# The first MLP product of a mixer block by Strassen's algorithm: seven 256-token block products per pair of column tiles in place of eight

## The chip, the cores and the metric

The kernel runs on one core of one Trainium2 chip. The metric is the device time of one execution in microseconds (us), as the median of several runs. The engines are named as in the profile: PE is TensorE (its matmuls), PEld the loading of weights into TensorE, DVE is VectorE, ACT is ScalarE, POOL is GpSimd, and SP is SyncE, which here issues the weight loads from HBM (DMAs).

## The reference

The reference is one layer of a hybrid block on x of 512 tokens by 1024 channels, in float32: four mixer branches, gates, an output projection, and then an MLP. The change touches only the MLP, which is

```python
h2 = rms_norm(x, norm_mlp_pre)          # 512 x 1024
u = jax.nn.relu(h2 @ w_mlp_in)          # w_mlp_in: 1024 x 4096
x = x + rms_norm((u * u) @ w_mlp_out, norm_mlp_post)
```

## The kernel before

Activations are kept transposed, channels on the 128 partitions and tokens along the free axis. The contraction over 1024 channels is thus 8 blocks of 128, numbered k, and `KD` is 8.

**Float32 by three matmuls.** Every operand is split in two, a rounded part `hi` and the rest `lo` (`split`: ACT casts `hi` on L157, DVE subtracts to get `lo` on L160). A product is then three matmuls, hi·hi, hi·lo and lo·hi (`mm3`, L256 to L258). The split of the normalised activation h2 is `h2h` and `h2l`, both kept in SBUF for all 512 tokens.

**The first MLP product.** `w_mlp_in` is taken in 32 tiles of 128 columns, numbered m. SP loads a tile (`raw`, 512 KB, four buffers), ACT and DVE split it into `whi` and `wlo` (three buffers each), and PE runs 8 k times 3 matmuls of 128 by 128 weights against all 512 tokens, 24 matmuls into one PSUM bank. `act_sq` follows: ACT applies Relu out of PSUM (L1117), and POOL squares in place (L1118). Results go to tiles `u2` of SBUF, eight m to a tile. The first four tiles (`NHALF`) are done in two halves of 256 tokens, because the last 128 tokens are still being normalised: first all four tiles on tokens 0 to 255, then all four on tokens 256 to 511.

**The late normalisation.** `norm_split` makes h2 from one 128-token block. For the last block (`late`) the order is: ACT sums the squares (L281), PE transposes the unscaled block (L293), ACT computes `rstd` (L273, L274), PE spreads `rstd` (L301), DVE scales (L304), ACT casts `h2h` (L306) and DVE subtracts `h2l` (L307).

**The second MLP product** (`rowproj` with `u_split`) takes u² back from the `u2` tiles, splits it two m at a time, and streams rows of `w_mlp_out`.

The order on each engine is not written out by hand around the change. It follows the order of the code, moved by a scheduler according to priorities, and buffers come from pools in rotation (`bufs`).

Of the kernel before, what the change touches and what calls it, by code (L numbers as in the profile page):

```python
# [120 lines left out]
def hybrid_mixer_kernel(ctx, tc, I, out):  # L121
# [15 lines left out]
    def ps_acc():  # L137
        return psp.tile([P, 512], F32, name="acc", tag="acc", bufs=2)
# [96 lines left out]
    def w_split(rv, where=None, eng=dve):  # L235
        wp, wb, tag = where or (wpool, 3, "w")
        hi = wp.tile([P, 1024], F32R, name="whi", tag=tag + "hi", bufs=wb)
        lo = wp.tile([P, 1024], F32R, name="wlo", tag=tag + "lo", bufs=wb)
        shape = rv.shape
        n = 1  # L240
        for d in shape[1:]:
            n *= d
        if len(shape) == 3:
            hv = hi[:, 0:n].rearrange("p (k c) -> p k c", k=shape[1])
            lv = lo[:, 0:n].rearrange("p (k c) -> p k c", k=shape[1])
        else:
# [27 lines left out]
        act.activation(out=r, in_=r, func=AF.Exp, scale=-0.5)  # L274
        return r

    def norm_split(src, gain, dh, dl, t, sq, late=False, first=None):


        ssq = tiny("ssq")  # L280
        a0 = act.activation(out=sq, in_=src, func=AF.Square, accum_out=ssq)  # L281
        r = rms_cols(ssq, D, "rstd")
        if not late:
            d0 = dve.tensor_scalar(out=sq, in0=src, scalar1=r, scalar2=None, op0=ALU.mult)
            if first:
# [729 lines left out]
    def m_tile(name, dt):  # L1015
        return mpool.tile([P, KD, S], dt, name=name, tag="mbig", bufs=2)
# [34 lines left out]
    def big2(name, dt):  # L1051
        return ph2.tile([P, KD, S], dt, name=name, tag="big2", bufs=2)
# [50 lines left out]
    def fin1(t, ps):  # L1103
        post_norm(ps, gpost, x1[:, t])
        sq = ph2.tile([P, D], F32, name="y", tag="y", bufs=2)
        norm_split(x1[:, t], V_MLP, h2h, h2l, t, sq, t == NT - 1)

    spare, uspl = (ph2, NSPARE, "w"), (ph2, 2, "u")
    rowproj(I["w_out"][0], KD, TAIL1, lambda k: (mh[:, k], ml[:, k]),
# [8 lines left out]
        pool.tensor_tensor(out=dst, in0=dst, in1=dst, op=ALU.mult)  # L1118

    w1 = I["w_mlp_in"][0]  # L1120
    for m in range(DFF // P):
        if m % 8 == 0:
            u2.append(big2("u2", F32) if m < 16 else m_tile("u2b", F32))
        if m < NHALF:
            continue
        if m == NHALF:
            first = [(ps_sm() if a else ps_acc(), w_split(raw_cols(w1, a * P), spare if a == 3 else None)) for a in range(NHALF)]
            for half in range(2):
                for a in range(NHALF):
                    proj(first[a][1], h2h, h2l, slice(256 * half, 256 * half + 256), first[a][0], half == 0)  # L1130
            for a in range(NHALF):
                act_sq(first[a][0], a)
# [79 lines left out]
```

## Time and profile before

| what | value |
| --- | --- |
| median of 3 runs | 885.64 us |
| lowest and highest run | 885.21 and 886.63 us |
| the profiled execution, its time | 884.56 us |
| the profiled execution, its span | 882.9 us |
| mean granted TensorE clock | 0.999 of full speed |

The span runs from the first to the last instruction of the profiled execution, and 1.7 us of its time lie around it. The profiled execution is 1.08 us under the median. "Granted clock" is the share of full TensorE speed that the throttle allowed. In the rows of a trace, times are us from the start of the span, and a matmul's shown duration includes the time until its last result, so that consecutive matmuls overlap in it.

### The profile page before, as it was taken

What the parts mean: (1) busy time and instruction counts of PE and PEld (TensorE: products, weight loads), DVE (VectorE), ACT (ScalarE), POOL (GpSimd) and SP (SyncE); (2) the same over time, 40 slices, a digit from 0 to 9 for tenths busy, and PEclk for the clock granted to TensorE, in tenths of its full rate; (3) what the DMA queues carried; (4) which work ended last, traced back from release to release, by engine and by line L of the source; (5) the groups of instructions that cost most, each with busy time, mean ns of one, the idle gap of its engine ahead of it and who ended that gap; (6) DMA issues with size and microseconds to landing.
All of it is one profiled execution on the core that took longest, in us unless ns stands there. A gap on an engine that the chain in (4) does not pass through costs nothing.

```text
span 882.9 us, 11119 instructions
## 1 busy us (share of the span) xinstructions
PE 866.5 (98%) x4407; PEld 712.9 (81%) x4407; DVE 437.9 (50%) x705; ACT 391.9 (44%) x667; POOL 117.7 (13%) x113
## 2 busy tenths in 40 slices
PE   7999999999999999999999999999999999999997
PEld 6987778987777778888888789888888888888885
DVE  6488798446885775344435575222222333333334
ACT  6346653425996755544443454322222332222222
POOL 3200020110000003022214002232222200000000
PEclk9999999999999999999999999999999999999999
DMA  8333253601220113333323803333333433333202
GB/s 264 102 104 95 60 114 89 128 25 52 67 85 26 48 48 97 96 95 96 97 95 110 271 27 93 96 96 96 97 96 101 128 106 99 104 96 103 75 1 95
DMA packets 123667, 83.24 MB, mean 94 GB/s; under 512 B 19472, under 2 KB 115744, under 8 KB 123616
## 3 DMA queue, kind: packets, MB, share of 16 engines
q1 hardware_dynamic: 117696, 77.03, 30.0%
q10 hardware_dynamic: 5696, 4.73, 1.7%
q0 software_dynamic: 224, 0.79, 0.3%
q8 instruction: 34, 0.56, 0.3%
q14 instruction: 17, 0.14, 0.1%
HBM read 79.63 MB, written 2.88 MB: 93 GB/s over the span
## 4 chain that ended last, share of the span: by engine, by line
PE 87%; DVE 6%; ACT 2%; POOL 2%; DMA 2%; issue 1%; ACTq 0%; SPq 0%; DVEq 0%; POOLq 0%
PE acc L258 53%; PE b L258 24%; PE b L817 2%; DVE wlo L160 1%; DVE qkvT L440 1%; PE b L847 1%; PE b L838 1%; DMA raw<-in_w_out_dram 1%; ACT whi L157 1%; PE b L646 1%; DMA raw<-in_w_in_dram 1%; PE b L293 1%; POOL gate L1042 1%; POOL wlo L160 1%; DVE dec L483 0%
## 5 line engine op out<-in xcount | busy, mean ns | idle before, releaser
L160 DVE TENSOR_TENSOR wlo<-raw,whi 128x1024 fp32r<-128x1024 f32 x134 | 171.6, 1284 | 257.7 <-ACT whi L157 257.5
L157 ACT CAST whi<-raw 128x1024 fp32r<-128x1024 f32 x136 | 142.8, 1053 | 274.6 <-PE acc L258 237.8
L258 PE MATMUL acc<-hh,wlo 128*128 128x512 f32 x368 | 145.8, 396 | 0.8 <-DVE wlo L160 0.8
L258 PE MATMUL acc<-hh,whi 128*128 128x512 f32 x368 | 146.2, 397 | 0.0
L258 PE MATMUL acc<-hl,whi 128*128 128x512 f32 x368 | 145.1, 394 | 0.0
L258 PE MATMUL acc<-h2l,whi 128*128 128x512 f32 (+1 forms) x240 | 91.7, 382 | 0.0
L258 PE MATMUL acc<-h2h,whi 128*128 128x512 f32 (+1 forms) x240 | 91.7, 382 | 0.0
L258 PE MATMUL acc<-h2h,wlo 128*128 128x512 f32 (+1 forms) x240 | 91.7, 382 | 0.0
L258 PEld LDWEIGHTS acc<-hh,wlo 128*128 128x128 f32 x368 | 69.2, 188 | 16.5 <-issue 1.6
L258 PEld LDWEIGHTS acc<-hh,whi 128*128 128x128 f32 x368 | 69.2, 188 | 14.9 <-issue 1.6
L258 PEld LDWEIGHTS acc<-hl,whi 128*128 128x128 f32 x368 | 69.2, 188 | 13.8 <-issue 0.4
L258 PE MATMUL b<-wlo,whi 128*128 128x512 f32 x192 | 74.7, 389 | 0.0
L258 PE MATMUL b<-whi 128*128 128x512 f32 x192 | 74.7, 389 | 0.0
L258 PE MATMUL b<-whi,wlo 128*128 128x512 f32 x192 | 74.6, 390 | 0.0
L258 PEld LDWEIGHTS acc<-h2h,whi 128*128 128x128 f32 x240 | 45.1, 188 | 8.8
L258 PEld LDWEIGHTS acc<-h2h,wlo 128*128 128x128 f32 x240 | 45.1, 188 | 8.7
L258 PEld LDWEIGHTS acc<-h2l,whi 128*128 128x128 f32 x240 | 45.1, 188 | 8.7
L1042 POOL TENSOR_TENSOR gate<-gate 128x512 f32<-128x512 f32 x16 | 22.6, 1418 | 198.2 <-DVE gate L1040 198.2
L258 PEld LDWEIGHTS b<-whi,wlo 128*128 128x128 f32 x192 | 36.0, 188 | 7.9 <-DVE wlo L160 0.4
L258 PEld LDWEIGHTS b<-whi 128*128 128x128 f32 x192 | 36.0, 188 | 7.5
L258 PEld LDWEIGHTS b<-wlo,whi 128*128 128x128 f32 x192 | 36.0, 188 | 7.4
L1118 POOL TENSOR_TENSOR u<-u 128x512 f32<-128x512 f32 x16 | 25.7, 1606 | 110.2 <-ACT u L1117 110.1
(322 smaller groups left out, 1461.2 us busy)
## 6 DMA issues: line engine op xcount, KB each, us to landing
raw<-in_w_gate_dram SPq DMA_DIRECT2D x32, 512.0 KB, 3.9
raw<-in_w_mlp_in_dram SPq DMA_DIRECT2D x32, 512.0 KB, 4.1
raw<-in_w_mlp_out_dram SPq DMA_DIRECT2D x32, 512.0 KB, 3.5
raw<-in_w_in_dram SPq DMA_DIRECT2D x23, 512.0 KB, 3.7
raw<-in_w_branch_up_dram SPq DMA_DIRECT2D x8, 512.0 KB, 3.8
raw<-in_w_out_dram SPq DMA_DIRECT2D x8, 512.0 KB, 3.5
x_t<-in_x_dram SPq DMA_DIRECT2D x4, 512.0 KB, 7.6
x<-in_x_dram ACTq DMA_DIRECT2D x1, 2048.0 KB, 11.9
```

The lines of the kernel that those rows point to most:

```text
L157: c = act.copy(out=hi, in_=src)
L160: eng.tensor_tensor(out=lo, in0=src, in1=hi.bitcast(F32), op=ALU.subtract)
L258: pe.matmul(out=ps, lhsT=a, rhs=b, start=first and i == 0, stop=last and i == 2, skip_group_check=True)
L293: pe.transpose(out=ps[:, k * P:(k + 1) * P], in_=(src if late else sq)[:, ks], identity=ident)
L440: dve.scalar_tensor_tensor(out=y[:, sh:], in0=ps[:, 0:S - sh], scalar=vec(V_CONV + 6 * j + m), in1=y[:, sh:], op0=ALU.mult, op1=ALU.add)
L646: pe.matmul(out=pv[:, j], lhsT=av[h][:, j], rhs=src[:, j], start=j == 0, stop=j == NT - 1, skip_group_check=True)
L817: pe.matmul(out=ps[:, at_[j]:at_[j] + n], lhsT=qT[e][0:rows, j * P:n], rhs=kT[e][0:rows, 0:n], start=j == js[0], stop=j == js[-1], skip_gr ...
L838: pe.transpose(out=pst[:, k * P:(k + 1) * P], in_=pr[:, k * P:(k + 1) * P], identity=ident)
L847: made.append(pe.matmul(out=psb[C * e:C * e + C, i * P:(i + 1) * P], lhsT=vt(k, 2 * p + e), rhs=pts[e][:, at_[j] + k * P:at_[j] + (k + 1) ...
L1042: pool.tensor_tensor(out=g, in0=g, in1=gts[4 * m + i - 1], op=ALU.add)
L1118: pool.tensor_tensor(out=dst, in0=dst, in1=dst, op=ALU.mult)
```

## The change

The 32 column tiles are now: four in two halves as before, tiles 4 and 5 as before (`NPLAIN = 6`), and the other 26 as 13 pairs. A pair of tiles (256 columns of the weights) and the 1024 channels in two halves make the weights a 2 by 2 matrix of blocks (`A[i][k]`, i the tile, k the half of the channels, each 512 channels by 128 columns), and h2 in two halves of channels and two halves of tokens is another (`B`, each 512 channels by 256 tokens). Their product takes eight block products in the plain way, and seven with Strassen's form with 15 sums: four sums of weight blocks (S1 to S4), four of activation blocks (T1 to T4, made once), and seven that combine products.

- h2 is now kept in float32 as well (`h2f`, a new argument `full` of `norm_split`), for all tokens. T1 to T4 are made from it in place, and each is split like any operand.
- For each pair, DVE makes S1 to S4 in place in the two `raw` tiles. A11 and A12, the two blocks of the first tile, are split together (`x`); A22 is split into a `y` buffer (`yw`); the four S are split two to a `whi`/`wlo` buffer.
- A block product is `part`: 4 k times 3 matmuls on 256 tokens, 12 matmuls. PE's order for one pair is p1 with A11, p6 (S2·T2), p5 (S1·T1), p1 again with A12 into the same bank, p7 (S3·T3), p3 (S4·B11), and p7 again with A22·T4 into the same bank.
- Five sums of products are DVE instructions that read PSUM: `sa`, `sb` and three of the four output blocks `o`. ACT copies p1 to `s1` in SBUF before p1 is continued, and applies Relu to each block. `s1`, `sa`, `sb` and `o[1][1]` have high priority in the scheduler.
- The square of u for these 26 tiles is on ACT (`Square`, one instruction for a tile) instead of POOL.

```diff
@@ norm_split
-    def norm_split(src, gain, dh, dl, t, sq, late=False, first=None):
+    def norm_split(src, gain, dh, dl, t, sq, late=False, first=None, full=None):
-            dst = sq[:, 512 * g:512 * g + 512].rearrange("p (k c) -> p k c", k=4) if late else pv
+            dst = (full[:, 4 * g:4 * g + 4, t * P:(t + 1) * P] if full is not None else
+                   sq[:, 512 * g:512 * g + 512].rearrange("p (k c) -> p k c", k=4) if late else pv)
...
+    diff(B[0][0], B[0][1], B[0][0])
+    T1 = rows_split(B[0][0], uspl)
+    diff(B[0][1], B[1][1], B[0][1])
+    diff(B[1][1], B[1][1], B[0][0])
+    T2 = rows_split(B[1][1], uspl)
+    T3 = rows_split(B[0][1], spare)
+    diff(B[1][0], B[1][0], B[1][1])
+
+    for m in range(NHALF, NPLAIN):
         act_sq(proj(w_split(raw_cols(w1, m * P)), h2h, h2l), m)
+    T4 = rows_split(B[1][0], spare)
...
+    def part(ps, w, t, start=True):
+        for k in range(KH):
+            mm3(ps, w[0][:, k], w[1][:, k], t[0][:, k], t[1][:, k], start and k == 0, k == KH - 1)
...
+        x = wt("x")
+        split(x[0], x[1], r[0])
+        z_ = ph2.tile([P, D], F32R, name="yw", tag="y", bufs=2).rearrange("p (z k c) -> p z k c", z=2, k=KH)
+        z = (z_[:, 0], z_[:, 1])
+        split(z[0], z[1], A[1][1])
+        diff(A[1][1], A[1][0], A[1][1], ALU.add)
+        diff(A[1][0], A[0][0], A[1][0])
+        diff(A[0][0], A[1][1], A[0][0])
+        diff(A[0][1], A[0][1], A[0][0])
+        got = []
+        for pair in ((A[0][0], A[1][1]), (A[1][0], A[0][1])):
+            e = wt("e")
+            for i, src in enumerate(pair):
+                ks = slice(KH * i, KH * i + KH)
+                split(e[0][:, ks], e[1][:, ks], src)
+                got.append((e[0][:, ks], e[1][:, ks]))
...
+        p1, p6, p5, p7, p3 = [bank() for _ in range(5)]
+        part(p1, A11, block(0, 0))
+        s1 = sz("s1")
+        with tc.high_priority():
+            act.copy(out=s1, in_=p1)
+        part(p6, S2, T2)
+        sa = sz("sa")
+        with tc.high_priority():
+            diff(sa, p6, s1, ALU.add)
+        part(p5, S1, T1)
+        sb = sz("sb")
+        with tc.high_priority():
+            diff(sb, p5, sa, ALU.add)
+        part(p1, A12, block(1, 0), False)
+        act.activation(out=o[0][0], in_=p1, func=AF.Relu)
+        part(p7, S3, T3)
+        with tc.high_priority():
+            diff(o[1][1], p7, sb, ALU.add)
+        part(p3, S4, block(1, 1))
+        diff(o[0][1], p3, sb, ALU.add)
+        part(p7, A22, T4, False)
+        diff(o[1][0], p7, sa, ALU.add)
+        for i, j in ((0, 1), (1, 1), (1, 0)):
+            act.activation(out=o[i][j], in_=o[i][j], func=AF.Relu)
+        for i in range(2):
+            d_ = u2[(m + i) // 8][:, (m + i) % 8]
+            act.activation(out=d_, in_=d_, func=AF.Square)
```

**PE in the steady part.** These are the rows on PE around the start of one column tile before the change, the end of one tile and the start of the next. The names are out<-activation,weights, and a row's end names the engines whose semaphores it waits on (the number behind an engine's name is only the semaphore's).

```order
L258 MATMUL acc<-h2h,wlo 128x512
L258 MATMUL acc<-h2h,whi 128x512 [waits Activation_49]
L258 MATMUL acc<-h2l,whi 128x512
L258 MATMUL acc<-h2h,wlo 128x512 [waits DVE_49]
L258 MATMUL acc<-h2h,whi 128x512
```

After the change, this is PE from the end of p5 through the second part of p1 (`b_5143<-h2h`), p7 with S3·T3 (`b_5146<-thi,whi`), p3 (`b_5147`) and the beginning of the second part of p7 (`b_5146<-thi,yw`), for one pair; rows that go on with a product are left out.

```order
L259 MATMUL acc<-thi,wlo 128x256
L259 MATMUL b_5143<-h2h,whi 128x256 [waits Activation_49]
...
L259 MATMUL b_5146<-thi,whi 128x256
...
L259 MATMUL b_5146<-thi,wlo 128x256 [waits DVE_49]
...
L259 MATMUL b_5147<-h2h,whi 128x256
...
L259 MATMUL b_5147<-h2h,wlo 128x256 [waits DVE_49]
...
L259 MATMUL b_5147<-h2h,wlo 128x256
L259 MATMUL b_5146<-thi,yw 128x256 [waits DVE_49]
L259 MATMUL b_5146<-tlo,yw 128x256
```

Where a tile before began with one wait for ACT (`whi`) and one for DVE (`wlo`), the second part of p1 now waits for ACT (the copy `s1` out of its bank), and the second part of p7 waits for DVE (the sum that reads the same bank).

**DVE in the steady part.** Before the change DVE had one row for each tile, `L160 TENSOR_TENSOR wlo<-raw,whi 128x1024`, so two for a pair. After it, these rows follow each other in one pair (`wlo` 128x1024 is the split of `x` for the next pair, `wlo` 128x512 that of an S, `raw<-raw` a sum S, `u_4982` an output block, with `sb` and `sa` as inputs).

```order
L1148 TENSOR_TENSOR sa<-acc,s_5160 128x256 [waits PE_49,Activation_49]
L1148 TENSOR_TENSOR sb<-acc,sa 128x256 [waits DVE_49,PE_49]
L161 TENSOR_TENSOR wlo<-raw,whi 128x1024 [waits Activation_49]
L161 TENSOR_TENSOR wlo<-raw,whi 128x512 [waits PE_49,Activation_49]
L1148 TENSOR_TENSOR raw<-raw 128x512 [waits DVE_49]
L1148 TENSOR_TENSOR u_4982<-b_5146,sb 128x256 [waits PE_49]
L1148 TENSOR_TENSOR raw<-raw 128x512 [waits DVE_49]
L161 TENSOR_TENSOR wlo<-raw,whi 128x512 [waits Activation_49]
L1148 TENSOR_TENSOR u_4982<-b_5147,sb 128x256 [waits PE_49]
L161 TENSOR_TENSOR wlo<-raw,whi 128x512 [waits Activation_49]
L1148 TENSOR_TENSOR u_4982<-b_5146,sa 128x256 [waits PE_49]
L161 TENSOR_TENSOR wlo<-raw,whi 128x512 [waits Activation_49]
```

Between `sb` and the sum that reads p7's bank (`u_4982<-b_5146,sb`) stand the split of the next pair's `x`, the split of its S1 and its difference S3.

**ACT at the late normalisation.** Before the change, ACT's rows from the sum of squares of the last 128 tokens to the casts of h2 are these.

```order
L281 ACTIVATE y,ssq<-x_4267 128x1024 [waits DVE_49]
L273 ACTIVATE rstd<-ssq,eps_col 128x1 [waits Activation_49]
L274 ACTIVATE rstd<-rstd 128x1 [waits Activation_49]
L306 CAST h2h<-y 128x4x128 [waits DVE_49] x2
L157 CAST whi<-raw 128x1024 [waits DMAHW5_49,PE_49]
```

After the change the same place reads so (`yw` is the cast of A22 of the first pair, whose weight tile comes by the DMA that it waits for; `thi` are casts of T).

```order
L282 ACTIVATE y,ssq<-x_4267 128x1024 [waits DVE_49,PE_49]
L158 CAST yw<-raw 128x512 [waits DMAHW1_49]
L274 ACTIVATE rstd<-ssq,eps_col 128x1 [waits Activation_49]
L275 ACTIVATE rstd<-rstd 128x1 [waits Activation_49]
L308 CAST h2h<-h2f 128x4x128 [waits DVE_49] x2
L158 CAST thi<-h2f 128x1024 [waits DVE_49] x2
```

One cast, with a wait for a DMA, now stands between the sum of squares and `rstd`.

## Rows read from the trace of the kernel before

**Rows 1.** The page: busy time of each engine; the chain that ended last, by engine.

```profile
PE 866.5 (98%) x4407; PEld 712.9 (81%) x4407; DVE 437.9 (50%) x705; ACT 391.9 (44%) x667; POOL 117.7 (13%) x113
...
PE 87%; DVE 6%; ACT 2%; POOL 2%; DMA 2%; issue 1%; ACTq 0%; SPq 0%; DVEq 0%; POOLq 0%
```

**Rows 2.** Stretches: us, then PE, PEld, DVE, ACT, POOL busy, clock, DMA share, GB/s.

```profile
524.40:549.60 25.20, 25.20 (x211) 25.10 (x211) 15.23 (x22) 12.19 (x22) 4.16 (x3) 1.00 0.36 105
549.60:701.90 152.30, 152.30 (x673) 126.08 (x673) 37.74 (x30) 44.48 (x58) 45.41 (x29) 1.00 0.34 100
701.90:876.30 174.40, 174.37 (x769) 143.74 (x767) 60.57 (x59) 50.54 (x64) 1.59 (x1) 1.00 0.25 84
```

**Rows 3.** The chain that ended last, 524 to 715 us: start, us, what.

```profile
534.52 0.18 PE b L301
...
538.05 2.88 PE acc L258 x24
540.93 8.64 PE b L258 x72
549.58 152.35 PE acc L258 x672
```

**Rows 4.** Groups of instructions, 560.4 to 701.9 us: shapes, count, busy, mean ns, idle before.

```profile
L258 PE MATMUL acc<-h2h,wlo 128*128 128x512 f32 x209 | 81.3, 389 | 0.0
...
L160 DVE TENSOR_TENSOR wlo<-raw,whi 128x1024 fp32r<-128x1024 f32 x27 | 33.6, 1246 | 107.8 <-ACT whi L157 107.8
L157 ACT CAST whi<-raw 128x1024 fp32r<-128x1024 f32 x28 | 29.6, 1056 | 104.2 <-PE acc L258 104.2
L1118 POOL TENSOR_TENSOR u2b<-u2b 128x512 f32<-128x512 f32 x15 | 23.9, 1592 | 57.7 <-ACT u2b L1117 57.7
```

**Rows 5.** Groups of instructions on PE, 540.8 to 549.5 us, where matmuls are 256 wide.

```profile
L258 PE MATMUL b<-h2h,wlo 128*128 128x256 f32 x24 | 6.8, 283 | 0.0
```

**Rows 6.** DVE in order of time, 484 to 560 us: start, us, what, count.

```profile
485.44 4.63 DVE L160 TENSOR_TENSOR wlo<-raw,whi 128x1024 fp32r<-128x1024 f32 x4 [2.03 <-ACT whi L157]
...
511.09 1.28 DVE L307 TENSOR_TENSOR h2l<-b,h2h 128x512 fp32r<-128x512 f32 x2
...
528.83 1.22 DVE L160 TENSOR_TENSOR wlo<-raw,whi 128x1024 fp32r<-128x1024 f32 x1
...
533.79 1.29 DVE L297 TENSOR_TENSOR y<-b,vecs 128x512 f32<-128x512 f32 x2 [1.22 <-ACT y L281]
535.00 1.28 DVE L304 TENSOR_TENSOR y<-y,b 128x512 f32<-128x512 f32 x2
536.36 1.29 DVE L307 TENSOR_TENSOR h2l<-y,h2h 128x512 fp32r<-128x512 f32 x2
...
549.48 1.77 DVE L160 TENSOR_TENSOR wlo<-raw,whi 128x1024 fp32r<-128x1024 f32 x1 [0.21 <-ACT whi L157]
...
555.94 1.22 DVE L160 TENSOR_TENSOR wlo<-raw,whi 128x1024 fp32r<-128x1024 f32 x1 [1.44 <-ACT whi L157]
```

**Rows 7.** Groups of DVE instructions, whole span: a 256-wide sum out of PSUM.

```profile
L658 DVE TENSOR_TENSOR ATs<-XD,b 64x256 f32<-64x256 f32 x8 | 3.3, 419 | 2.5 <-PE b L646 2.3
```

**Rows 8.** Groups of ACT instructions, whole span: a 512-wide cast, a 256-wide copy.

```profile
L157 ACT CAST sqh<-sq 128x512 fp32r<-128x512 f32 x11 | 6.8, 617 | 0.3 <-DVE sql L160 0.3
...
L384 ACT COPY gv<-acc 128x256 f32<-128x256 f32 x4 | 1.5, 374 | 1.1 <-PE acc L258 1.1
```

**Rows 9.** ACT in order of time, 526 to 560 us: start, us, what.

```profile
532.61 1.06 ACT L281 ACTIVATE y<-x 128x1024 f32<-128x1024 f32 x1 [2.63 <-DVE x L1101]
...
533.79 0.30 ACT L273 ACTIVATE rstd<-ssq,eps_col 128x1 f32<-128x1 f32 x1
534.12 0.20 ACT L274 ACTIVATE rstd<-rstd 128x1 f32<-128x1 f32 x1
...
554.85 1.06 ACT L157 CAST whi<-raw 128x1024 fp32r<-128x1024 f32 x1 [1.61 <-PE acc L258]
```

**Rows 10.** The page's DMA issues: count, size, median us to landing.

```profile
raw<-in_w_mlp_in_dram SPq DMA_DIRECT2D x32, 512.0 KB, 4.1
```

More of the change, by code (lines that the diff above doesn't have):

```diff
@@ L27 @@
 NHALF = 4
+NPLAIN = 6
 G0 = 2
@@ L1059, in hybrid_mixer_kernel @@
     h2l = big_tile("h2l", F32R)
+    h2f = big2("h2f", F32)
     banks["ring"] = ("b0", "b1", "b2", "b3", "b4", "b5")
@@ L1105, in fin1 @@
         sq = ph2.tile([P, D], F32, name="y", tag="y", bufs=2)
-        norm_split(x1[:, t], V_MLP, h2h, h2l, t, sq, t == NT - 1)
+        norm_split(x1[:, t], V_MLP, h2h, h2l, t, sq, t == NT - 1, None, h2f)
     spare, uspl = (ph2, NSPARE, "w"), (ph2, 2, "u")
@@ L1120, in hybrid_mixer_kernel @@
     w1 = I["w_mlp_in"][0]
[L1121 to L1132, printed above, removed]
-        act_sq(proj(w_split(raw_cols(w1, m * P)), h2h, h2l), m)
+    u2.append(big2("u2", F32))
@@ new lines, in hybrid_mixer_kernel, with rows_split @@
+    first = [(ps_sm() if a else ps_acc(), w_split(raw_cols(w1, a * P), spare if a == 3 else None)) for a in range(NHALF)]
+    for half in range(2):
+        for a in range(NHALF):
+            proj(first[a][1], h2h, h2l, slice(256 * half, 256 * half + 256), first[a][0], half == 0)
+    for a in range(NHALF):
+        act_sq(first[a][0], a)
+    KH = KD // 2
+    B = [[h2f[:, KH * i:KH * i + KH, 256 * j:256 * j + 256] for j in range(2)] for i in range(2)]
+    def rows_split(src, where):
+        wp, wb, tag = where
+        hi = wp.tile([P, 1024], F32R, name="thi", tag=tag + "hi", bufs=wb).rearrange("p (k c) -> p k c", k=KH)
+        lo = wp.tile([P, 1024], F32R, name="tlo", tag=tag + "lo", bufs=wb).rearrange("p (k c) -> p k c", k=KH)
+        split(hi, lo, src)
+        return hi, lo
@@ new lines, in diff @@
+    def diff(out, a, b, op=ALU.subtract):
+        dve.tensor_tensor(out=out, in0=a, in1=b, op=op)
+    diff(B[0][0], B[0][1], B[0][0])
[6 more added lines that the diff above has]
+    for m in range(NHALF, NPLAIN):
+        act_sq(proj(w_split(raw_cols(w1, m * P)), h2h, h2l), m)
+    T4 = rows_split(B[1][0], spare)
+    u2 += [big2("u2", F32)] + [m_tile("u2b", F32) for _ in range(2)]
@@ new lines, in hybrid_mixer_kernel, with bank @@
+    block = lambda i, j: tuple(z[:, KH * i:KH * i + KH, 256 * j:256 * j + 256] for z in (h2h, h2l))
+    ring8 = [lambda: ps_sm("b0"), lambda: ps_sm("b1"), lambda: ps_sm("b2"), lambda: ps_sm("b3"), lambda: ps_sm("b4"),
+             lambda: ps_sm("b5"), ps_acc, ps_acc]
+    turn = [0]
+    def bank():
+        turn[0] += 1
+        return ring8[(turn[0] - 1) % 8]()[:, 0:256]
+    def part(ps, w, t, start=True):
+        for k in range(KH):
+            mm3(ps, w[0][:, k], w[1][:, k], t[0][:, k], t[1][:, k], start and k == 0, k == KH - 1)
@@ new lines, in w_sums, with wt @@
+    def w_sums(m):
+        r = [raw_cols(w1, (m + i) * P) for i in range(2)]
+        A = [[v[:, KH * i:KH * i + KH] for i in range(2)] for v in r]
+        def wt(name):
+            return [wpool.tile([P, 1024], F32R, name="w" + z, tag="w" + z, bufs=3).rearrange("p (k c) -> p k c", k=KD)
+                    for z in ("hi", "lo")]
+        x = wt("x")
[14 more added lines that the diff above has]
+                got.append((e[0][:, ks], e[1][:, ks]))
+        A11, A12 = [(x[0][:, KH * i:KH * i + KH], x[1][:, KH * i:KH * i + KH]) for i in range(2)]
+        S2, S1, S3, S4 = got
+        return A11, A12, z, S1, S2, S3, S4
@@ new lines, in hybrid_mixer_kernel @@
+    sz = lambda name: ph2.tile([P, 256], F32, name=name, tag="sz", bufs=4)
+    for m in range(NPLAIN, DFF // P, 2):
+        A11, A12, A22, S1, S2, S3, S4 = w_sums(m)
+        o = [[u2[(m + i) // 8][:, (m + i) % 8, 256 * j:256 * j + 256] for j in range(2)] for i in range(2)]
+        p1, p6, p5, p7, p3 = [bank() for _ in range(5)]
[25 more added lines that the diff above has]
+            act.activation(out=d_, in_=d_, func=AF.Square)
```

## Prediction, made before the changed kernel was run

> **What bounds the kernel now.** I read the page first: PE is busy for 98% of the span, DVE for half of it, ACT for less, and PE holds 87% of the chain that ended last [rows 1]. An average says nothing of one stage, so I then took the stretches [rows 2]. The plain part of the first MLP product runs from 549.60 to 701.90 us: PE is busy for all 152.30 us, the granted clock is 1.00 (the 2.4 GHz level), DVE works for 37.74 us and ACT for 44.48. The chain of that stretch is one unbroken piece of PE, 672 matmuls in 152.35 us [rows 3]. So the stage lasts as long as its matmuls take, and DVE and ACT have room: DVE's 27 splits there were preceded by 107.8 us of idleness [rows 4]. The same holds for what follows, the second product, with PE busy for 174.37 of 174.40 us [rows 2], so time saved here reaches the end.
>
> **What the change removes and adds on PE.** The price of a matmul is its distance to the next, not its shown duration (389 ns at 512 wide [rows 4], 283 ns at 256 wide [rows 5]), since they overlap. At 512 wide it is 152.35 / 672 = 0.2267 us. At 256 wide the kernel before has a stretch of its own, the second halves of the first four tiles: 72 matmuls over three banks in 8.64 us and 24 in 2.88 us [rows 3], 0.1200 us in both, bank changes included. Half the width thus costs 53% of the time: 13.3 ns at each matmul do not shrink (0.2267 = x + 512 y and 0.1200 = x + 256 y give x = 13.3 ns).
>
> - Before, a pair of tiles has 48 matmuls of 512: 48 x 0.2267 = 10.88 us.
> - After, seven products of 12 matmuls of 256: 84 x 0.1200 = 10.08 us.
> - Saved: 0.80 us for a pair, 13 x 0.802 = **10.4 us** in all. One eighth of the work is gone, 7.4% of the time.
>
> In that 256-wide stretch the loading of weights was busy for 25.10 of 25.20 us [rows 2]; 0.1200 already includes it. The 256-wide stretches ran at clock 1.00 too, and PE has no new pause if the steps below hold.
>
> A rule to weigh here: the Trainium skill, TensorE: Matmul & The Clock Gate, section Back-to-back issue gap, gives N/2.4 + 2.5 ns between matmuls, a fixed part of 2.5 ns in place of my 13.3. By it a pair would go from 10.36 to 9.17 us, 15.4 us saved in all. The trace does not agree at either width (0.1200 and 0.2267 against 0.109 and 0.216), and the sum goes by the rows.
>
> **DVE and ACT in a pair (10.08 us).** DVE has 15 instructions where it had two: a split of 1024 columns, nine of 512 (five splits, four sums), five of 256 out of PSUM. The shown durations are 1.23, 0.69 (two in 1.28, so 0.60 apart) and 0.42 [rows 6, 7]; four of 1024 in a row take 4.63, so 1.13 apart [rows 6]. In all 1.13 + 9 x 0.60 + 5 x 0.42 = 8.6 us by distance, 1.23 + 9 x 0.69 + 5 x 0.42 = 9.5 us by duration. Both lie under 10.08, with 0.5 to 1.5 us to spare. ACT has a cast of 1024 (1.05), five of 512 (0.62), five copies or Relus of 256 (0.37) and two squares (no row here; taken as 0.62, like the cast): 7.2 us [rows 4, 8]. POOL loses the squares of these tiles, 1.59 us each [rows 4], which were off the path.
>
> **The one tight wait.** The second part of p7 goes into a bank that DVE must have read (the output block o11), and on DVE the next pair's split of x, a split of S1 and the difference S3 stand ahead of that sum. I walk it from a, the start of p1's second part. In the built program the next pair's x takes the buffer that p5, the product before, used last; p5's last use of it ends at about a + 0.04 (0.28 after a start at a - 0.24 [rows 5]). From an engine's end to the next one's start I take 0.03 (554.85 + 1.06 to 555.94 [rows 6, 9]).
>
> - ACT casts x from a + 0.07 to 1.12; DVE splits x from 1.15, S1 from 2.28, makes S3 from 2.88 and o11 from 3.48 to 3.90; PE may go on at 3.93.
> - PE comes there after three products of 12 x 0.12: a + 4.32. Margin 0.39 us; with full durations in place of distances o11 ends at 4.18, margin 0.11.
>
> So I take no stall. The rest of the loop has room: S2's split ends near a + 5.1 and is needed at 7.2, the copy s1 is done 2.3 us before p1's bank is reopened, and the last weight sums end near a + 8.5, before the next pair's sa can start at 8.8.
>
> **The start of the stage.** T1 to T4 add four differences and four splits of 1024 columns, 8 x 1.13 = 9.0 us on DVE and four casts on ACT. They fall between 537 and 553 us, where PE works through halves and plain tiles with weights split ahead: DVE and ACT were busy for 15.23 and 12.19 of 25.20 us there [rows 2]. They fit, and pair 1 needs them only after 560 us.
>
> What does not fit is one cast. On ACT the first pair's `yw` cast stands between the sum of squares of the last 128 tokens and `rstd`. Its weight tile is loaded into the buffer that DVE frees at 530.05 (the split at 528.83 [rows 6]), and with 4.1 us to land [rows 10] it is there at 534.15, not at 533.76, when ACT would take it. The cast adds 0.62: `rstd` starts at 534.8 in place of 533.79 and ends at 535.35 in place of 534.32 [rows 9]. PE's spreading of `rstd`, at 534.52 [rows 3], had 0.2 to spare, so PE waits for 0.85 us. On DVE the scaling moves from 535.00 to 535.85, the difference for T1 comes in behind it (1.13), and `h2l` starts near 538.2 and is ready at 538.9; PE, late by 0.85, wants it at 538.05 + 0.85 + 0.12 = 539.0 [rows 3, 6]. No second wait. I take **0.9 us** with PE's restart; bounds 0.4 (a tile that landed early leaves the cast less 0.2 to spare) and 1.8 (0.4 later, and a T1 difference that is not hidden).
>
> **Sum.** Profiled execution: 884.56 - 10.4 + 0.9 = 875.1 us. The median of the runs is 1.08 above that execution: 885.64 - 9.5 = **876.1 us**.
>
> **Rivals.**
>
> 1. *Small stalls in every pair*, 0.1 to 0.3 us at o11, at sa or at the restart behind a wait. For it: a margin of 0.39 with a floor of 0.11, and seven waits on PE in a pair where there were four. Against it: PE had no gap in 672 matmuls although every tile waits for ACT and DVE. 13 x 0.1 to 0.3 gives 877.4 to 880.0 us.
> 2. *The chain ahead of o11 is late: slower than before.* If x cannot be cast until p1's second part is over (a buffer freed 1.44 us later), or DVE takes as much longer for its three instructions, o11 ends at a + 5.34 and PE goes on at 5.37 in place of 4.32, a wait of 1.05 us in each of the 12 pairs that have a successor. That gives 876.1 + 12.6 = 888.7 us. It decides from a delay of 0.39 + 9.5/12 = 1.2 us. For it: a split of 1024 columns took 1.77 us at 549.48 in place of 1.23 [rows 6]. Against it: one such instruction gives 0.54 alone, POOL no longer squares beside it, and the buffer is the one that p5 frees.
> 3. *DVE becomes the bound.* Its 15 instructions have 0.5 us to spare by duration. A pause of 0.1 us behind each makes 11.0 us a pair and 876.1 + 13 x 0.96 = 888.6 us. Against it: four splits stood 1.13 apart, closer than their shown 1.23 [rows 6], so consecutive instructions overlap. The Trainium skill, VectorE: DVE Perf Modes, section The DRAIN you can't avoid, has every DVE instruction followed by a pause of its duration less 0.27 us; by it a pair would take 15.0 us and the kernel some 940. The rows of consecutive splits show no such pause.
> 4. *More is saved.* If the part of a matmul that does not shrink with its width were smaller in the new stretch, say 256-wide matmuls 0.110 us apart, a pair would take 9.24 us and the kernel 876.1 - 13 x 0.84 = 865.2. Against it: the 96 matmuls of that width went at 0.1200 [rows 3]. The page of the skill named first, TensorE: Matmul & The Clock Gate, would have it so.
>
> **How the numbers follow.** Forecast 0.74; small stalls 0.13; chain late 0.06; DVE bound 0.03; more saved 0.02; stalls that just eat the gain 0.02. A measurement of this kernel tells about 0.2% (1.8 us) from no change. Faster by more than that: 0.74 + 0.13 + 0.02 = 0.89; within it 0.02; slower 0.09. The range takes the forecast with its bounds (a matmul distance 0.001 us off moves 1.1 us; the start 0.4 to 1.8) and the small stalls: 874.0 to 880.5 us, which leaves out about 0.13.
>
> **What would show it.** Right: the 26 tiles take 131 us as 1092 matmuls 0.120 us apart; PE has no wait for DVE or ACT between pairs; DVE is busy for 8.5 to 9.5 us of each 10.08; PE stands still for somewhat under 1 us before the `rstd` transpose near 534.5; the second product and the tail are as before. Wrong: a period over 10.1 us with PE waiting for DVE ahead of p7's second part (rival 2), or DVE without idle time (rival 3), or distances other than 0.120 us (rival 4).

## The result, and the profile after

The changed kernel takes 876.39 us (median of 4 runs, 875.75 to 876.59) against 885.77 us for the kernel before (4 runs): a ratio of 0.9896, 95% interval 0.9882 to 0.9910. The forecast was 876.1 us with a range of 874.0 to 880.5.

The profiled execution took 875.75 us with a span of 874.0. These are the two lines of its page that answer to [rows 1]: busy time by engine, and the chain that ended last.

```profile
PE 858.1 (98%) x4875; PEld 728.8 (83%) x4875; DVE 529.9 (61%) x882; ACT 441.4 (50%) x788; POOL 75.6 (9%) x87
...
PE 86%; DVE 6%; DMA 2%; ACT 2%; POOL 2%; issue 1%; ACTq 0%; SPq 0%; DVEq 0%; POOLq 0%
```

VectorE went from 437.9 to 529.9 us of work, TensorE is still the chain. The stretches below, of the changed kernel, answer to [rows 2]: the 13 pairs and the second product (us, then PE, PEld, DVE, ACT, POOL busy, clock, DMA share, GB/s).

```profile
561.30:692.30 131.00, 131.00 (x1091) 130.88 (x1090) 109.06 (x187) 86.56 (x167) 1.05 (x1) 1.00 0.39 108
692.30:867.00 174.70, 174.70 (x775) 144.54 (x774) 62.58 (x63) 51.78 (x67) 0.00 (x0) 1.00 0.27 90
```

The 26 tiles of the pairs take 131.00 us, all of it TensorE, at clock 1.00, and VectorE works for 109.06 of them, 8.4 us a pair. The second product takes as long as before (174.70 us here, 174.40 before). TensorE's waits from 524 to 700 us, the whole product with its start, are one line (engine and line, what it waited for, us, times, longest):

```profile
PE b L303 <- ACT rstd L275: 0.4, 1, 0.4
```

No pair made TensorE wait. The chain of the changed kernel, 524 to 715 us, answers to [rows 3] (start, us, what):

```profile
529.65 5.24 DMA raw<-in_w_mlp_in_dram
...
534.91 0.62 ACT yw L158
535.53 0.21 ACT rstd L274
...
535.76 0.21 ACT rstd L275
...
536.34 3.35 PE b L259 x28
...
551.21 10.91 PE acc L259 x48
```

Behind 551.21 us it is TensorE alone; the 48 matmuls of the two plain tiles take 10.91 us. Ahead of 536.34 it runs through a weight load, the cast `yw` and `rstd` (and, from 536.02, TensorE's spreading of `rstd`): the place that the prediction named.

One pair on VectorE, the cast of x on ScalarE, and on TensorE the first matmuls of p1's second part and of p7's second part, as the timeline of the changed kernel has them (start, us, what, and idle time before):

```profile
607.75 1.83 DVE L161 TENSOR_TENSOR wlo<-raw,whi 128x1024 fp32r<-128x1024 f32 x2 [0.53 <-ACT whi L158]
609.49 0.68 DVE L1148 TENSOR_TENSOR raw<-raw 128x512 f32<-128x512 f32 x1
610.09 0.42 DVE L1148 TENSOR_TENSOR u<-acc,sb 128x256 f32<-128x256 f32 x1
```

```profile
606.67 1.05 ACT L158 CAST whi<-raw 128x1024 fp32r<-128x1024 f32 x1 [1.86 <-PE acc L259]
```

```profile
606.59 0.28 PE L259 MATMUL b<-h2h,whi 128*128 128x256 f32 x1
...
610.91 0.28 PE L259 MATMUL acc<-thi,yw 128*128 128x256 f32 x1
```

So a, the start of p1's second part, is 606.59. The prediction walked x's split to a + 1.15, S3 to 2.88 and o11 to 3.48 until 3.90. The trace has 1.16 (607.75), 2.90 (609.49) and 3.50 until 3.92 (610.09 and 0.42). TensorE's next product starts at 610.91, a + 4.32 as predicted.

**Where 8.8 us of the span went, stage by stage.** The starts of four instructions split the two spans (last gate product on VectorE, first matmul on h2, tile 4, last matmul of the product), tile 4 as the chain has it, the others from the timelines:

| start at, us | before | changed | difference of the stage |
| --- | --- | --- | --- |
| last gate product | 477.56 | 479.69 | +2.13 (code that the change leaves alone) |
| first matmul on h2 | 524.45 | 525.50 | -1.08 |
| tile 4 | 549.58 | 551.21 | +0.58 |
| last matmul of the first product | 701.53 | 692.87 | -10.29 |
| end of the span | 882.85 | 874.04 | -0.15 |

The first two stages are not the change's. The experiment with two halves below, whose code up to there is that of the kernel before, reaches the last gate product at 480.10, and the twelve profiles other than that of the kernel before lie between 478.1 and 480.1. And the stage up to the first matmul on h2 takes either 45.7 to 45.9 or 46.7 to 47.0 us in the profiled executions of this study, with the same kernel on both sides (45.81, 46.94 and 45.75 for the changed one). In the six long ones TensorE waits in it for VectorE's part of a weight split (0.8 us) and for ScalarE's (0.5 to 0.6 us); in the seven short ones no such wait is over 0.2 us. What the change made is thus +0.58 at the start and -10.29 in the product; the rest is variation from execution to execution, of 1 to 2 us.

### The profile page after: what moved, and what is told of

Read it like the earlier page. It is cut to its first block, busy times and chain, and to the rows that moved or that the text cites. A ratio compares the mean times of both kernels' runs of the same rounds, so it can differ in the third digit from the quotient of the medians.

```text
span 874.0 us, 12382 instructions
## 1 busy us (share of the span) xinstructions
PE 858.1 (98%) x4875; PEld 728.8 (83%) x4875; DVE 529.9 (61%) x882; ACT 441.4 (50%) x788; POOL 75.6 (9%) x87
## 3 DMA queue, kind: packets, MB, share of 16 engines
HBM read 79.63 MB, written 2.88 MB: 94 GB/s over the span
## 4 chain that ended last, share of the span: by engine, by line
PE 86%; DVE 6%; DMA 2%; ACT 2%; POOL 2%; issue 1%; ACTq 0%; SPq 0%; DVEq 0%; POOLq 0%
PE acc L259 41%; PE b L259 34%; PE b L819 2%; DMA raw<-in_w_mlp_in_dram 2%; DVE wlo L161 2%; DVE qkvT L442 1%; PE b L849 1%; PE b L840 1%; PE b L648 1%; ACT whi L158 1%; DMA raw<-in_w_in_dram 1%; POOL gate L1044 1%; POOL wlo L161 1%; PE b L495 1%; PE b L294 1%
## 5 line engine op out<-in xcount | busy, mean ns | idle before, releaser
L161 DVE TENSOR_TENSOR wlo<-raw,whi 128x1024 fp32r<-128x1024 f32 (+1 forms) x173 | 190.2, 1109 | 146.6 <-ACT whi L158 146.3
L158 ACT CAST whi<-raw 128x1024 fp32r<-128x1024 f32 (+1 forms) x175 | 159.7, 921 | 211.7 <-PE acc L259 143.6
L259 PE MATMUL b<-h2l,whi 128*128 128x256 f32 x168 | 47.7, 284 | 0.0
L259 PE MATMUL b<-h2h,wlo 128*128 128x256 f32 x168 | 47.6, 283 | 0.0
L259 PE MATMUL b<-h2h,whi 128*128 128x256 f32 x168 | 47.5, 283 | 0.0
L1148 DVE TENSOR_TENSOR raw<-raw 128x512 f32<-128x512 f32 x52 | 37.3, 717 | 0.9
L259 PE MATMUL b<-thi,whi 128*128 128x256 f32 x116 | 32.8, 283 | 0.0
L259 PE MATMUL b<-tlo,whi 128*128 128x256 f32 x116 | 32.8, 283 | 0.0
L259 PE MATMUL b<-thi,wlo 128*128 128x256 f32 x116 | 32.8, 283 | 0.0
```

What stands on the lines that cost most here:

```text
L158: c = act.copy(out=hi, in_=src)
L161: eng.tensor_tensor(out=lo, in0=src, in1=hi.bitcast(F32), op=ALU.subtract)
L259: pe.matmul(out=ps, lhsT=a, rhs=b, start=first and i == 0, stop=last and i == 2, skip_group_check=True)
L1148: dve.tensor_tensor(out=out, in0=a, in1=b, op=op)
```

## The experiments

Each median is of 4 or 5 runs (9 where said). "Before" is the kernel before on the same chip: 885.27 us beside the halves, the seven pairs, the first later cast and the squares on GpSimd; 885.89 beside the changed kernel's second profile, the small delay, the second split of x and the 14 pairs; 885.74 beside the changed kernel's third profile, the later cast again and the 14 pairs with GpSimd idle. Since the early stages vary by more than most effects, the traces are also compared over the product alone, from the start of its first matmul to the start of its last:

| kernel | first | last | us between | median |
| --- | --- | --- | --- | --- |
| before | 524.45 | 701.53 | 177.08 | 885.77 |
| changed | 525.50 | 692.87 | 167.37 | 876.39 |
| changed, second profile | 525.97 | 692.90 | 166.93 | 876.19 |
| changed, third profile | 523.89 | 690.97 | 167.08 | 874.36 |
| A22's cast later | 525.72 | 692.64 | 166.92 | 875.30 |
| A22's cast later, again | 525.41 | 692.33 | 166.92 | 875.60 |
| halves, no Strassen | 525.77 | 711.27 | 185.50 | 894.53 |
| seven pairs | 526.80 | 698.52 | 171.72 | 879.83 |
| squares on GpSimd | 525.52 | 692.47 | 166.95 | 875.46 |
| small delay of o11 | 525.43 | 693.93 | 168.50 | 876.80 |
| x split twice | 526.41 | 705.73 | 179.32 | 887.74 |
| 14 pairs | 525.87 | 694.00 | 168.13 | 877.18 |
| 14 pairs, GpSimd idle | 524.54 | 691.21 | 166.67 | 874.00 |

**The width alone: eight products of 256 in place of 512.**

```diff
-        act_sq(proj(w_split(raw_cols(w1, m * P)), h2h, h2l), m)
+        if m < 6:
+            act_sq(proj(w_split(raw_cols(w1, m * P)), h2h, h2l), m)
+            continue
+        wt, ps = w_split(raw_cols(w1, m * P)), ps_acc()
+        for half in range(2):
+            proj(wt, h2h, h2l, slice(256 * half, 256 * half + 256), ps, half == 0)
+        act_sq(ps, m)
```

> The kernel before, with column tiles 6 to 31 done in two halves of 256 tokens each, so eight products of 12 matmuls of 256 columns for a pair where Strassen has seven; no other change. Theory (0.1200 us from matmul to matmul at 256 wide, 0.2267 at 512, so 13.3 ns that do not shrink): a tile takes 48 x 0.1200 = 5.76 in place of 5.44 us, 26 x 0.32 = 8.3 us more than before, about 894.0 us; the eighth product is then worth 26 x 0.72 = 18.7 us. Rival (a fixed part of 2.5 ns in the new stretch): 26 x 0.06 = 1.6 us more than before, about 887.3 us, and the stage's distances near 0.110 us.

It took 894.53 us, 1.0095 of before (1.0076 to 1.0113). The chain of this kernel has the 28 tiles in one piece:

```profile
550.90 160.66 PE acc L258 x1296
```

Two plain tiles are 48 x 0.2267 = 10.88 us of it, so 1248 matmuls of 256 took 149.78, 0.1200 each. The product is 8.42 us longer than before (8.3 expected). The part of a matmul that does not shrink with its width is confirmed where it matters, and the rival of a small fixed part is refuted: halving the width costs 8.4 us over 26 tiles, and leaving out the eighth product gives back 185.50 - 166.93 = 18.6 us.

**Fewer pairs.**

```diff
-NPLAIN = 6
+NPLAIN = 18
...
+        if m == 6:
+            T4 = rows_split(B[1][0], spare)
+            u2 += [big2("u2", F32)] + [m_tile("u2b", F32) for _ in range(2)]
```

> The changed kernel with tiles 6 to 17 in the plain way and only tiles 18 to 31 in seven pairs. Theory (0.80 us saved in each pair, and a cost of the start that does not depend on the number of pairs): 6 pairs fewer cost 4.8 us, so 881.2 us. Rival (the gain comes once, from the squares' move to ScalarE or from the order of the start): within 1 us of 876.4 us. In the trace, plain tiles take 5.44 us each and pairs 10.08.

It took 879.83 us, 0.9932 of before (0.9916 to 0.9949), 1.4 us under what I wrote. Its chain:

```profile
552.06 76.19 PE acc L259 x336
```

336 matmuls in 76.19 us are 14 tiles at 5.44 us. The product takes 171.72 us, 4.80 more than with 13 pairs and no wait at the start (166.92): 0.80 us for each of the six pairs. My 881.2 was built on a time with the wait at the start, which this kernel does not have (its first pair starts at 628.25 in place of 562.12, 66 us later, and its cast of A22 comes later too); the rest of the 1.4 us is within the variation of the early stages. The gain is made in each pair, not once.

**The cast ahead of rstd.**

`last[0][0]` is the last cast of h2, which `fin1` keeps; `split` orders its own cast behind it.

```diff
+        if m == NPLAIN:
+            behind.append(last[0][0])
         split(z[0], z[1], A[1][1])
```

> The changed kernel with one order added on ScalarE: the cast of A22 of the first pair comes behind the last cast of h2 instead of ahead of rstd; nothing else is asked for. Theory (the start's cost is that cast and the DMA it waits for): rstd of the last 128 tokens starts right behind the sum of squares, TensorE's wait of 0.4 to 0.6 us ahead of the spreading of rstd is gone, and the time falls by about 0.5 us, from 876.4 to about 875.9 us. Rival (the start is late because h2 is kept in float32 and VectorE's rows of the normalisation stand in another order): the wait ahead of rstd's spreading goes, but TensorE waits as long a little later, for h2l, and the time stays at 876.4.

> The first experiment again (the cast of A22 of the first pair behind the last cast of h2), beside the changed kernel on the same chip. Theory: 0.4 to 0.9 us under the changed kernel, because rstd's wait for a DMA and a cast is gone. Rival: no difference over 0.3 us.

The first took 875.30 us (0.9882 of before, 0.9867 to 0.9897), the second 875.60 (0.9891, 0.9873 to 0.9908) where the changed kernel beside it took 874.36 (0.9877, 0.9857 to 0.9897). The times do not tell the two apart, and the second did not come out as expected: it lies 1.24 us over the changed kernel beside it, where 0.4 to 0.9 us under it was expected. Its profile reached the last gate product 1.5 us later than that kernel's (479.64 against 478.13), in code that is the same in both. The traces do tell them apart. ScalarE in the changed kernel at that place:

```profile
533.45 1.06 ACT L282 ACTIVATE y<-x 128x1024 f32<-128x1024 f32 x1 [1.97 <-DVE x L1104]
...
534.91 0.62 ACT L158 CAST yw<-raw 128x512 fp32r<-128x512 f32 x1 [0.32 <-DMA raw<-in_w_mlp_in_dram]
535.44 0.29 ACT L274 ACTIVATE rstd<-ssq,eps_col 128x1 f32<-128x1 f32 x1
```

And in the experiment, where rstd follows the sum of squares at once:

```profile
533.66 1.06 ACT L282 ACTIVATE y<-x 128x1024 f32<-128x1024 f32 x1 [1.97 <-DVE x L1104]
...
534.85 0.29 ACT L274 ACTIVATE rstd<-ssq,eps_col 128x1 f32<-128x1 f32 x1
...
537.63 0.61 ACT L158 CAST yw<-raw 128x512 fp32r<-128x512 f32 x1
```

The wait for `rstd` is gone, as the theory had it, and TensorE does not wait later, so the rival falls. But the gain is only what the wait cost: 167.37 against 166.92 us in one pair of traces, 0.45, and 0.01 and 0.16 against the two other profiles of the changed kernel.

**The changed kernel twice more.**

> The changed kernel once more, beside the next three on the same chip, as their yardstick. Every theory expects the time of the first result, 876.4 us give or take 1 us, 9 to 10 us under the kernel before. In its trace the stretch from the tile 4 to the end of the pairs takes 141.9 us again; what differs is when the first loads of x land and how long TensorE waits for the weights of the output projection.

> The changed kernel, as the yardstick on the chip of these three. 876.4 us give or take 1 us; from the tile 4 to the end of the pairs 141.9 us.

They took 876.19 us (0.9892 of before, 0.9874 to 0.9910) and 874.36 us. The last lies 2 us under the first result and outside what was expected, with 872.59 to 876.08 us in its runs. ScalarE in the second profile:

```profile
533.91 1.06 ACT L282 ACTIVATE y<-x 128x1024 f32<-128x1024 f32 x1 [1.96 <-DVE x L1104]
...
534.97 0.60 ACT L158 CAST yw<-raw 128x512 fp32r<-128x512 f32 x1
535.48 0.29 ACT L274 ACTIVATE rstd<-ssq,eps_col 128x1 f32<-128x1 f32 x1
```

Here the load had landed when ScalarE came to it, and `yw` followed the sum of squares at once. The cast still put `rstd` off, but TensorE's spreading of it came only 0.10 us later behind the matmul ahead of it than before the change, too little to be listed as a wait. How long TensorE waits here thus differs from execution to execution: 0.53, 0.10 and 0.22 us in the three profiles of the changed kernel.

**Squares back on GpSimd.**

```diff
-            act.activation(out=d_, in_=d_, func=AF.Square)
+            pool.tensor_tensor(out=d_, in0=d_, in1=d_, op=ALU.mult)
```

> The changed kernel with the squares of the 26 tiles back on GpSimd. Theory (TensorE sets the time; VectorE has about 1.5 us of room in a pair and GpSimd's two squares fall where VectorE makes the next but one pair's sums, behind o11): VectorE's instructions beside a square get longer, 0.69 to as much as 1 us, VectorE is busy for over 9 us in 10.08, and the time stays within 0.5 us of 876.4. Rival (the squares' move to ScalarE was needed, since the margin ahead of o11 is 0.39 us and a split beside a square took 0.54 us longer before): TensorE waits for VectorE ahead of p7's second part, 0.1 to 0.5 us a pair, 1 to 6 us in all, 877.5 to 882.5 us.

It took 875.46 us, 0.9884 of before (0.9866 to 0.9901). Its stretch of the pairs, and VectorE beside two squares that GpSimd did from 602.16 to 604.65:

```profile
561.00:692.00 131.00, 131.00 (x1092) 130.88 (x1091) 124.47 (x188) 74.18 (x143) 30.91 (x25) 1.00 0.38 108
```

```profile
602.48 1.27 DVE L161 TENSOR_TENSOR wlo<-raw,whi 128x512 fp32r<-128x512 f32 x1
603.67 1.52 DVE L161 TENSOR_TENSOR yw<-raw,yw 128x512 fp32r<-128x512 f32 x1
```

Two splits of 512 columns took 1.27 and 1.52 us in place of 0.69, more than the 1 us that was expected at most, and VectorE was busy for 124.47 us instead of 109.06, but the squares fall behind o11, and TensorE did not wait. Moving them to ScalarE was not needed for the time.

**The margin ahead of o11, from both sides.** Both kernels hold the orders of TensorE and VectorE to those of the changed kernel (a dependency without a semaphore from each product to the next and from S3 to o11); they differ in what is added. The small delay:

```diff
                 split(e[0][:, ks], e[1][:, ks], src)
+                if m > NPLAIN and src is A[1][1]:
+                    kh = slice(KH * i, KH * i + 2)
+                    in_order([dve.tensor_tensor(out=e[1][:, kh], in0=src[:, 0:2], in1=e[0][:, kh].bitcast(F32), op=ALU.subtract), o11[-1]])
```

The second split of x:

```diff
         split(x[0], x[1], r[0])
+        dve.tensor_tensor(out=x[1], in0=r[0], in1=x[0].bitcast(F32), op=ALU.subtract)
```

> The changed kernel with one more VectorE instruction in each of 12 pairs, 128 by 256 (a repeated part of the split of S1, same values), put right ahead of the sum o11 that reads p7's bank; the orders of TensorE and VectorE are held to those of the changed kernel. Theory (o11 ends at a + 3.90 and TensorE wants p7's bank at a + 4.32): o11 ends 0.33 us later, at 4.23 to 4.28, TensorE still does not wait, and the time is that of the changed kernel. Rival (the margin was used up already, or a wait near its limit costs a restart): TensorE waits 0.1 to 0.3 us in each pair, 1 to 4 us in all.

> The changed kernel with the split of x of the next pair done twice on VectorE (same values), and with o11 held behind it and behind the difference S3, and the products of TensorE held in their order. Theory (the chain of VectorE ahead of o11 sets the start of p7's second part once it is over 0.39 us longer): o11 ends at about a + 5.03, TensorE goes on at 5.06 in place of 4.32, waits 0.74 us in each of 12 pairs, 8.9 us in all, and the gain of the change is nearly gone: about 885.3 us (883.5 to 887). Rival (TensorE's wait is made up for, since VectorE has 1.5 us of room in a pair): the time stays within 1 us of the changed kernel.

The small delay took 876.80 us, 0.9895 of before (0.9875 to 0.9914). VectorE and TensorE in one of its pairs:

```profile
610.40 0.42 DVE L1209 TENSOR_TENSOR wlo<-raw,whi 128x256 fp32r<-128x256 f32 x1
610.74 0.42 DVE L1150 TENSOR_TENSOR u<-acc,sb 128x256 f32<-128x256 f32 x1
```

```profile
611.09 0.28 PE L261 MATMUL b<-h2h,wlo 128*128 128x256 f32 x1
611.21 0.38 PE L261 MATMUL acc<-thi,yw 128*128 128x256 f32 x1
611.43 0.28 PE L261 MATMUL acc<-tlo,yw 128*128 128x256 f32 x1
```

o11 ends at 610.74 + 0.42 = 611.16, and the product is shown to start at 611.21, its nominal place 0.12 behind the matmul before. But the next matmul comes after 0.22 in place of 0.12. The rows of the weight loads say why, those of the changed kernel first:

```profile
610.79 0.19 PEld L259 LDWEIGHTS acc<-thi,yw 128*128 128x128 f32 x1
```

```profile
610.98 0.19 PEld L261 LDWEIGHTS b<-h2h,wlo 128*128 128x128 f32 x1
611.21 0.19 PEld L261 LDWEIGHTS acc<-thi,yw 128*128 128x128 f32 x1
```

In the changed kernel the weights of the product's first matmul are loaded from 610.79, 0.12 ahead of the matmul, at a + 4.20. With the small delay their turn was at 611.10, 0.12 behind the load before, but the load starts at 611.21, 0.05 behind o11's end. Read so, it is the load that waited for o11, for 0.11 us, and the room behind o11 ends at a + 4.15 (4.20 less 0.05) and not at 4.29: 0.23 us in place of the 0.39 that the prediction gave. The same 0.10 stands in all 12 pairs, 1.2 us; the product as a whole is 1.1 to 1.6 us longer than in the changed kernel. So here the rival is right on a small scale. That the load is what waits is read from these rows; no experiment moves the load alone.

The second split of x took 887.74 us (9 runs), 1.0026 of before (1.0016 to 1.0036): slower than the kernel before by 0.3%. TensorE at p7 in one of its pairs, and its waits for these sums:

```profile
604.39 0.28 PE L261 MATMUL b<-h2h,wlo 128*128 128x256 f32 x1
605.43 0.39 PE L261 MATMUL b<-thi,yw 128*128 128x256 f32 x1 [0.76 <-DVE u L1150]
605.65 0.28 PE L261 MATMUL b<-tlo,yw 128*128 128x256 f32 x1
```

```profile
PE b L261 <- DVE u2b L1150: 4.6, 6, 0.8
PE b L261 <- DVE u L1150: 3.0, 4, 0.8
PE acc L261 <- DVE u L1150: 0.8, 1, 0.8
PE acc L261 <- DVE u2b L1150: 0.8, 1, 0.8
```

```profile
601.35 1.83 DVE L161 TENSOR_TENSOR wlo<-raw,whi 128x1024 fp32r<-128x1024 f32 x2 [0.53 <-ACT whi L158]
603.09 1.22 DVE L1192 TENSOR_TENSOR wlo<-raw,whi 128x1024 fp32r<-128x1024 f32 x1
604.35 0.69 DVE L1150 TENSOR_TENSOR raw<-raw 128x512 f32<-128x512 f32 x1
604.96 0.75 DVE L1150 TENSOR_TENSOR u<-b,sb 128x256 f32<-128x256 f32 x2
```

These are 12 waits, one for each pair that has a successor. The second part of p1 starts at 600.19 here, which is a. The pairs are 11.10 us apart (x's split at 601.35 and 612.45), 1.02 more than 10.08, where I expected 0.74. o11 starts at 604.96, a + 4.77 in place of 4.61, mostly because S3 began 0.04 behind the second split's end, 1.26 after its start in place of the 1.13 at which such splits follow each other; TensorE went on 0.05 after o11's end in place of 0.03, and its next matmul came 0.10 late (the load of the weights started only with the shown start, at 605.43). That is 0.74 + 0.16 + 0.02 + 0.10 = 1.02. The rival (VectorE makes it up) is refuted, and the prediction's second rival is shown to be a real mechanism: o11 came 1.27 us later than in the changed kernel (a + 4.77 against 3.50), and that undoes the whole gain.

**One more pair, and one without GpSimd.**

```diff
-NPLAIN = 6
+NPLAIN = 4
```

This kernel and the next also have the later cast of A22 from above.

> The changed kernel with the cast of A22 of the first pair behind the last cast of h2 (as in the first experiment), and 14 pairs: tiles 4 and 5 are a pair too. Theory (0.80 us a pair, and the start has room for its sums): 0.8 us less for the pair and 0.5 us for the cast, about 1.3 us under the changed kernel on the same chip. Rival (the eight operations for T and the first pair's 15 on VectorE do not fit between the last split of h2 and the first pair, which now begins 11 us earlier): TensorE waits for VectorE in the first pair, 1 to 3 us, and the time is that of the changed kernel or over it.

It took 877.18 us, 0.9901 of before (0.9885 to 0.9917), not less than the changed kernel beside it (876.19): the rival came true. VectorE and TensorE in the first pair, and GpSimd's squares of the four first tiles:

```profile
557.62 3.53 DVE L161 TENSOR_TENSOR wlo<-raw,whi 128x1024 fp32r<-128x1024 f32 x2
561.07 0.41 DVE L1150 TENSOR_TENSOR u<-b,sb 128x256 f32<-128x256 f32 x1
```

```profile
560.06 0.28 PE L259 MATMUL b<-h2h,wlo 128*128 128x256 f32 x1
561.54 0.39 PE L259 MATMUL b<-thi,yw 128*128 128x256 f32 x1 [1.20 <-DVE u L1150]
```

```profile
544.03 16.57 POOL L1123 TENSOR_TENSOR u<-u 128x512 f32<-128x512 f32 x4 [60.47 <-ACT u L1122]
```

Two splits took 3.53 us where the changed kernel has 1.83, o11 ended at 561.48 and TensorE stood from 560.18 to 561.54. Four squares in 16.57 us are 4.14 each, against 1.3 to 2.1 for the same four in the changed kernel. Most of VectorE's instructions beside them kept their length, but these two splits did not. The next kernel takes the squares off GpSimd, and nothing else:

```diff
-        pool.tensor_tensor(out=dst, in0=dst, in1=dst, op=ALU.mult)
+        act.activation(out=dst, in_=dst, func=AF.Square)
```

> The kernel of the experiment with 14 pairs and the later cast of A22, with the squares of the first four tiles on ScalarE too, so that GpSimd squares nothing. Theory (there VectorE's split of x of the second pair took 3.5 us beside GpSimd's squares, o11 was late and TensorE waited 1.2 us in the first pair): the four squares are off GpSimd, the two splits take 1.8 us, TensorE's wait of 1.2 us is gone, and the time is 1.2 us under that experiment, about 1.3 us under the changed kernel. Rival (the first pair's wait comes from the number of VectorE's instructions ahead of it, not from GpSimd): TensorE waits about as long and the time is that of the changed kernel.

It took 874.00 us, 0.9873 of before (0.9856 to 0.9889). The same two splits:

```profile
556.29 1.83 DVE L161 TENSOR_TENSOR wlo<-raw,whi 128x1024 fp32r<-128x1024 f32 x2
```

1.83 us again, no wait of TensorE for o11, and a product of 166.67 us, the shortest here and 1.46 us under the kernel with GpSimd. So it was GpSimd's squares that lengthened the splits; that VectorE lengthened the squares in turn is seen side by side and not tested. By median it lies 0.4 us under the changed kernel beside it (874.36, whose runs spread over 3.5 us), where 1.3 was expected: the times do not tell them apart, the traces put it 0.3 to 0.7 us ahead.

Against the later cast with 13 pairs (166.92 us) the 14th pair gives only 0.25 us and not 0.80. In both kernels with 14 pairs five matmuls near the start of the first pair follow after 0.20 to 0.29 us in place of 0.12 (here between 549.87 and 553.70), 0.60 us in all, which is most of what is missing. Two of the five begin 0.05 us behind the end of a ScalarE instruction, a Relu out of a bank (550.67 + 0.59) and the copy `s1` (553.05 + 0.37): the first pair's start has no room for its work after all.

## Why the prediction was right

The forecast was 876.1 us and the result 876.39, with the mechanism as described. Point by point:

- **The saving on TensorE** (0.1200 us at 256 wide, 0.2267 at 512, 10.4 us in all): 131.00 us in place of 141.44. The experiments put it at 0.80 us a pair (seven pairs) and split it into 8.4 us lost by the width and 18.6 us gained by the eighth product.
- **VectorE's load** (8.6 us by distance, 9.5 by duration): 8.4 us a pair, just under the 8.5 to 9.5 that the prediction named as its sign. The distances were the right measure; the sum by distance still took the five sums out of PSUM at 0.42, and they follow at 0.34 (610.09 to 610.43). ScalarE was busy for 6.7 us a pair (86.56 / 13) where 7.2 was reckoned.
- **The wait ahead of o11**: right to 0.02 us in its times. What was wrong is the margin: it was counted to the matmul at a + 4.32, but by the rows of the small delay the load of its weights, 0.12 earlier, waits for o11 already, so that 0.23 of the 0.39 us was free. The second rival's mechanism is confirmed by the second split of x; its price for a delay was mis-sized too, 1.02 us a pair where the same reckoning gave 0.74.
- **The rest of the loop**: the last weight sums of a pair end at a + 9.04 (615.63) where the prediction had 8.5, and so sa starts at a + 8.96 and not at 8.8. Nothing waited for it here.
- **The start** (0.9 us): the mechanism was right, the size was off, in both of its terms. In three profiles the start was 0.58, 0.14 and 0.29 us longer than before (first matmul on h2 to tile 4: 25.71, 25.27 and 25.42 against 25.13). Counted from the sum of squares, `rstd` started 0.81, 0.39 and 0.52 us later than before (1.99, 1.57 and 1.70 against 1.18), where the prediction had 1.0. TensorE's spreading of it came 0.67, 0.24 and 0.36 us behind the matmul ahead of it against 0.14 before, so 0.53, 0.10 and 0.22 late: it had 0.28 to 0.30 us to spare. The prediction's "0.2 to spare" was taken from the chain, where the piece of the spreading begins at 534.52; the timeline has its start at 534.38, 0.06 behind rstd's end, so that the kernel before had hardly any. What room there was came with the order on TensorE, 13 matmuls behind the transposes in place of 10. The spreading before and after:

```profile
534.38 0.32 PE L301 MATMUL b<-cst,rstd 128*128 128x128 f32 x1
```

```profile
536.02 0.32 PE L303 MATMUL b<-cst,rstd 128*128 128x128 f32 x1 [0.39 <-ACT rstd L275]
```

- **The conversion from span to median** (1.08 us): it fits. The profiled execution of before was early by 2.13 us and then late by 1.08 beside that of the changed kernel, in code that the change does not touch, and the spans alone, 882.85 and 874.04, show 8.8 us where the product's stages show 9.7 to 10.2.
- **The closeness of the number**, 0.3 us, is in part luck: the start was priced 0.3 to 0.8 us too high, and the changed kernel's own medians, 876.39, 876.19 and 874.36, lie 2 us apart. What the runs bear out is the saving of 0.80 us a pair.
- **The two rules of the Trainium skill** that were weighed: the first (TensorE: Matmul & The Clock Gate, Back-to-back issue gap), which the section gives for an isolated matmul and the prediction applied to a stream, did not hold here, since distances were 0.1200 us in all 13 pairs and in the halves, not 0.109. The second (VectorE: DVE Perf Modes, The DRAIN you can't avoid) was taken too widely in the prediction: that section adds that "A next op that is not held starts earlier". The trace agrees with this addition: VectorE's instructions followed each other at 0.60 us for 0.69 shown, with no pause between.

Left open: what makes the first 20 us and the waits for split weights ahead of the first matmul on h2 differ by 1 to 2 us between executions was not tried.

## What to carry to other kernels

Here a matmul had a part that did not shrink with its width (13.3 ns by the distances at 256 and 512, the only two widths tried), so price a scheme that halves the width by distances at both widths: an eighth less work gave 7.4% of the time. A change that fills a second engine to 83% of the bound engine's time is safe only as far as the order on it allows: find the one instruction on which the bound engine waits, walk what stands ahead of it, and count its margin to the load of the weights and not to the matmul. Effects under 1 us are read from the stretch that makes them, since the rest of the kernel varies by more.

## What was not expected of the hardware

- Where o11 ended 0.05 us ahead of the turn of the matmul that waits for it, the load of that matmul's weights started 0.11 us late (at 611.21 in place of 611.10), and the next matmul followed after 0.22 us in place of 0.12.
- GpSimd's squares of 128 by 512, 1.3 to 2.1 us in the changed kernel, took 4.14 us each beside a VectorE without gaps, and a pair of VectorE's splits went from 1.83 to 3.53 us. With the same squares on ScalarE the splits took 1.83 us.
- Executions of the same code differ by about 2 us in the first 20 us: one VectorE sum of the first normalisation starts at 17.73 us in the profile of the kernel before, at 19.83 in that of the changed kernel, and at 18.07 in its third. The stage up to the first matmul on h2 has two lengths, about 1 us apart.
